# Differential attention on one core: the row squares taken earlier, the prompt's sums by products with ones, the last prompt one group sooner

## The chip, the core and the metric

The kernel runs on one core of a Trainium2 chip. Five engines work side by side, each through its own queue in order: TensorE (PE; its weight loads are shown apart as PEld), VectorE (DVE), ScalarE (ACT), GpSimd (POOL) and SyncE (SP), which issues most of the DMAs. The metric is the device time of one execution in microseconds (us); lower is better. The runs of the kernel before have a median of 2910.99 us.

## The reference, cut to what matters

One transformer layer for 256 prompt tokens and 2048 latent tokens, model width 1024. Attention has 4 heads; each head has two halves of 64 channels for queries and keys and one value of 128 channels. Latent queries read 512 cached and 2048 latent keys in one softmax; prompt queries read the 256 prompt keys.

```python
s = jnp.einsum('bqhmd,bkhmd->bhmqk', qblk, k).astype(jnp.float32) * scale
p = jax.nn.softmax(s, axis=-1)
a = p[:, :, 0] - lam * p[:, :, 1]                 # difference of the two halves
o = jnp.einsum('bhqk,bkhe->bqhe', a.astype(v.dtype), v)
...
a = rms_norm(attn, subln_g) * (1.0 - lam_init)    # per head, over its 128 channels
mix = jnp.concatenate([a.reshape(b, n, ATTN_WIDTH), four], axis=-1) @ w_out
x = x + g1 * mix
```

The per-head `rms_norm` is what most of the change is about: for every query the mean square over 128 channels of its output is needed.

## The kernel before

Before attention the kernel projects, normalises and rotates, and computes the Fourier half; after it come the out projection, and an MLP whose matmuls are combined so that seven products stand for eight. Between the parts there are no barriers: the work is one program, and attention's end overlaps the out projection's start.

**Attention.** `Head` holds the keys and values of one head, `Group` the work on 256 latent queries (two blocks j of 128), `Prompt` (a subclass of `Group`) that on the 256 prompt queries. There are 4 heads of 8 groups. All steps are put in a list with a time (`add(t, fn, ...)`, with T = 5.2 as the length of a row and u = T/5) and issued in the order of these times under `manual_schedule`; the times set the order alone. Synchronisation is derived from that order and from which tiles the instructions read and write.

A row of a group is one pass (j, half m) over the keys in blocks of 512:

- `fill`: two products give the scores of one block in a PSUM bank (L1081; tile S, five banks, tag "S").
- `rowmax` (L1086) takes the maximum of each block on VectorE, and `comb` (L1089) the maximum over the blocks.
- `exp` (L1105) on ScalarE writes the exponentials to SBUF (P0 or P1), and frees the bank. The scores of a row are made while the exponentials of the row before it are taken.
- `combine` (L1110 to L1121, VectorE and GpSimd) forms the difference of the two halves, scaled by the sums.

Six rows after its first, a group begins to turn its weights: `tr` transposes pairs of key blocks into a bank of tag "pt" (L1136; two banks), `ah` and `al` split them in a high and a low part (L1143 on ScalarE, L1148 on VectorE), and one row later `mul` multiplies them by the values (L1162 for the pairs kept in full precision, vf4 and vf14, and L95 to L97 for the others, three products each). The result gathers in columns 0 to 255 of one PSUM bank, po (`PRO()`), of which there is one.

When a group's products are complete, `o1` copies them to SBUF (oT, L1173), `o2` transposes them into columns 256 to 511 of the same bank (L1177), so that the queries lie on the partitions, and `o4` squares them with a sum along the row (L1183, two ACTIVATEs, each with a read of its accumulator). `o5` adds the epsilon term and raises to -1/2 on GpSimd (L1186, L92), `o6` and `o7` send the 256 numbers through DRAM to spread them over all partitions, `o8` (L1204) multiplies and `o9` (L1208) stores the group's output in `att`. Of the last group all from `o4` on is issued in the out projection (`LASTO`).

The prompt of a head runs between the rows of its groups 1 to 6, with scores and products in columns 256 to 511 of po. Its `o2` transposes into a bank of tag "pt" (L1265), and `o4` squares there (L1271).

In the times above, `o4` of a group stands at w + 8.5 u with w = base + 11 T + 1.0 u, which is 4.5 u into a row; the casts of that row (`ah`) stand at 3.3 and 3.8 u, and the value products of the following group (`mul`) at 3.9 u.

**The out projection** starts with 128 prompt tokens; their input mix0 is loaded by `mix0_load` (L1295) from `att[0]`, which the prompts of all four heads write, and split on VectorE (L1582, L1583).

Of the kernel before, what the change touches and what calls it, by code (L numbers as in the profile page):

```python
# [11 lines left out]
F32 = mybir.dt.float32  # L12
F32R = mybir.dt.float32r
AF = mybir.ActivationFunctionType
ALU = mybir.AluOpType
# [4 lines left out]
P = 128  # L20
# [6 lines left out]
H = 4  # L27
# [4 lines left out]
TSTEP, AVS = 5.2, 6  # L32
# [9 lines left out]
def body(tc, a, out):  # L42
    nc = tc.nc
    ctx = ExitStack()
    with ctx:
# [3 lines left out]
        def cst(name, shape, dt=F32):  # L49
            return const.tile(shape, dt, tag=name, name=name)  # L50
# [21 lines left out]
        ident = cst("ident", [P, P])  # L72
# [3 lines left out]
        ones = cst("ones", [P, 1])  # L76
# [14 lines left out]
        def pow_mhalf(dst, src, n):  # L91
            nc.gpsimd.tensor_tensor(dst, src, mhalf[:, :n], op=ALU.pow)  # L92
# [897 lines left out]
        with ExitStack() as c3_:  # L990
# [4 lines left out]
            at = c3_.enter_context(tc.tile_pool(name="a_t", bufs=2, reuse_waits="tile"))  # L995
# [4 lines left out]
            pT = c3_.enter_context(tc.tile_pool(name="a_pt", bufs=2, space=PSUM, reuse_waits="tile"))  # L1000
# [3 lines left out]
            @functools.cache  # L1004
            def PRO():

                return pPO.tile([P, 512], F32, tag="po", name="po")
# [32 lines left out]
            class Group:  # L1040
# [134 lines left out]
                def o2(self):  # L1175
                    for j in range(2):
                        nc.tensor.transpose(self.po[:, 256 + j * P:256 + j * P + P], self.oT[:, j * P:j * P + P], ident)  # L1177

                def o4(self):
                    osq = self.op.tile([P, P], F32, tag="osq", name=f"osq{self.nm}", bufs=1)  # L1180
                    self.oss = self.op.tile([P, 4], F32, tag="oss", name=f"oss{self.nm}")
                    for j in range(2):
                        nc.scalar.activation(osq, self.po[:, 256 + j * P:256 + j * P + P], AF.Square, accum_out=self.oss[:, j:j + 1])  # L1183

                def o5(self):
                    nc.gpsimd.tensor_add(self.oss[:, 0:2], self.oss[:, 0:2], self.s0e)  # L1186
                    pow_mhalf(self.oss[:, 2:4], self.oss[:, 0:2], 2)
# [22 lines left out]
            class Prompt(Group):  # L1210
# [47 lines left out]
                def o1(self):  # L1258
                    self.oT = f32(at.tile([P, 512], F32R, tag="ahp", name=f"oT{self.nm}", bufs=1))[:, 0:256]
                    nc.scalar.copy(self.oT, PRO()[:, 256:512])  # L1260

                def o2(self):
                    self.pt[1] = pT.tile([P, 512], F32, tag="pt", name=f"pt{self.nm}_o")[:, 0:256]
                    for j in range(2):
                        nc.tensor.transpose(self.pt[1][:, j * P:j * P + P], self.oT[:, j * P:j * P + P], ident)  # L1265

                def o4(self):
                    osq = at.tile([P, P], F32, tag="osq", name=f"osq{self.nm}", bufs=1)
                    self.oss = at.tile([P, 4], F32, tag="oss", name=f"oss{self.nm}")
                    for j in range(2):  # L1270
                        nc.scalar.activation(osq, self.pt[1][:, j * P:j * P + P], AF.Square, accum_out=self.oss[:, j:j + 1])  # L1271

            ev = []

            def add(t, fn, *args):
                ev.append((t, len(ev), fn, args))

            T = TSTEP
            u = T / 5.0
# [17 lines left out]
            for h in range(H):  # L1297
                hd, hp = Head(0, h), Head(1, h)
                base = h * 32 * T
                add(base - 18 * T + 0.7 if h else -3.04 * T, hd.load_k)  # L1300
                add(base - 14 * T + 0.7 if h else 0.9 * T, hd.load_v)
                add(base + 2 * T + 0.7, hp.load_k)
                add(base + 2 * T + 0.71, hp.load_v)
                gp = Prompt(hp, 0)
                G = [base + (AVS + 4 * g) * T for g in range(8)]
                add(G[1] - 3 * T, gp.qload)
                for j in range(2):
                    for m in range(2):
                        for t, fn in ((0.4, gp.scores), (0.85, gp.rowmax), (2.7, gp.exp)):
                            add(G[1 + 2 * j + m] + t * u, fn, j, m)  # L1310
                    add(G[2 + 2 * j] + 8 * u, gp.combine, j)
                for t, fn, *args in ((0.25, gp.tr, 0), (0.9, gp.ah), (1.4, gp.al), (17.0, gp.mul), (20.85, gp.o1), (24.2, gp.o2),
                                     (24.9, gp.o4), (25.6, gp.o5), (28.2, gp.o6), (32.7, gp.o7),
                                     (40.2, gp.o8), (43.0, gp.o9)):
                    add(G[5] + t * u, fn, *args)
                for g in range(hd.ng):
                    gr = Group(hd, g)
                    add(base - (4 if h or g > 1 else 3) * T + 0.6 * u if base else -3.03 * T, gr.qload)
                    for st in range(4):
                        j, m = divmod(st, 2)  # L1320
                        t0 = base + st * T
                        for b in range(hd.nbk):
                            add(t0 - T + (0.76 + 0.66 * b) * u, gr.fill, j, m, b)
                            add(t0 - T + (1.26 + 0.66 * b) * u, gr.rowmax, j, m, b)
                            add(t0 + 0.66 * b * u, gr.exp, j, m, b)
                        add(t0 - 0.45 * u, gr.comb, j, m)
                        if m:
                            add(t0 + (4.5 if gr.last and j else 5.9) * u, gr.combine, j)
                            if gr.last and j:
                                add(t0 + T + 5.3 * u, gr.combine_v, j)  # L1330
                    kbs = list(range(0, hd.nkt, 2))
                    for q in range(4):
                        w = base + (AVS + q) * T
                        if q % 2 == 0:
                            order = [kbs.pop(0) for _ in range(2)]
                            tr_t, ah_t, al_t = [0.7, 2.2], [3.3, 3.8], [4.6, 5.2]
                        else:
                            order = [kbs.pop(0) for _ in range(3)]
                            tr_t, ah_t, al_t = [0.7, 2.2, 3.86], [3.3, 3.8, 4.4], [None, 4.6, 5.2]
                        for n, kb in enumerate(order):  # L1340
                            add(w + tr_t[n] * u, gr.tr, kb)
                            add(w + (2.0 if gr.drain and kb == FULL[0] else ah_t[n]) * u, gr.ah, kb)
                            if al_t[n]:
                                add(w + al_t[n] * u, gr.al, kb)
                            add(w + T + (3.9 + 0.01 * n) * u, gr.mul, kb)
                            if q == 3 and not n:
                                add(w + 3.95 * u, gr.mul_part, kb)
                    w = base + (AVS + 5) * T + 1.0 * u
                    for t, fn in ((0, gr.o1), (0.4, gr.o2), (8.5, gr.o4), (9.2, gr.o5), (11.8, gr.o6), (16.3, gr.o7), (23.4, gr.o8), (26.0, gr.o9)):
                        if gr.last and t > 1:  # L1350
                            LASTO.append(fn)
                        else:
                            add(w + t * u, fn)
                    base += 4 * T
            add(base - 16 * T, load_wout)
            add(base + (AVS - 2) * T + 0.7 * u, mix0_load)
            with tc.manual_schedule():
                for _, _, fn, args in sorted(ev, key=lambda e: (e[0], e[1])):
                    fn(*args)
# [87 lines left out]
        WO5, HO, LO, hp = {}, {}, [], {}  # L1447
# [264 lines left out]
        with c5r, ExitStack() as c5:  # L1712
# [4 lines left out]
            PSB, U, G = {}, {}, {}  # L1717
# [152 lines left out]
            with tc.manual_schedule():  # L1870
                for n, (q, p) in enumerate(ITEMS):
# [21 lines left out]
                    ps = mms(q, p)  # L1893
                    fn, args = FINISH.get(n, (None, ()))
# [66 lines left out]
        with ExitStack() as c6:  # L1961
# [62 lines left out]
            with tc.manual_schedule():  # L2024
                pend, NM, loaded, KS = None, 7 * 24, 4, []
                for i in range(7):
                    for b in range(3):
                        ps = [pp.tile([P, 512], F32, tag="ps", name=f"ps{i}_{b}_{j}", bufs=6) for j in range(3)]
                        for k in range(16):
                            n, m = i * 16 + k, (i * 3 + b) * 8 + k // 2  # L2030
# [18 lines left out]
                            if (i, b) == (6, 2) and 9 <= k < 12:  # L2049

                                j = k - 9
                                u = U3[6 + j]
# [13 lines left out]
                for j in range(3):  # L2066
                    t = 6 + j
# [70 lines left out]
```

## Time and profile before

| | us |
|---|---|
| runs shown | 2908.22, 2910.99, 2912.67 (median 2910.99) |
| the profiled execution, its own time | 2909.53 |
| its span, first to last instruction | 2907.7 |
| granted TensorE clock over the span | 0.999 |

| engine | busy us | share of the span |
|---|---|---|
| PE | 2841.9 | 98% |
| PEld | 2446.2 | 84% |
| DVE | 1983.5 | 68% |
| ACT | 1535.3 | 53% |
| POOL | 1074.3 | 37% |

Attention's first combined maximum is at 520.75 us and its last at 1269.82; its last product ends at about 1297.

How to read the lines: a group of instructions is named by line, engine, operation, the tile written and the tiles read ("po<-ahs,Vs"), with buffer numbers left out; "s" at the end of a name is latent, "p" prompt. A line of the timeline starts with its start and its length in us; merged neighbours carry their count (x4). What stands in brackets is the idle time of the engine just before, and what ended it. A wait is put down to the releaser that came last. Matmuls are pipelined: a busy TensorE is not one at its peak, and the start of the weight load (PEld) is the sharper mark. L95 to L97 and L92 are lines of helpers.

### The profile page before, as it was taken

What the parts mean: (1) busy time and instruction counts of PE and PEld (TensorE: products, weight loads), DVE (VectorE), ACT (ScalarE), POOL (GpSimd) and SP (SyncE); (2) the same over time, 40 slices, a digit from 0 to 9 for tenths busy, and PEclk for the clock granted to TensorE, in tenths of its full rate; (3) what the DMA queues carried; (4) which work ended last, traced back from release to release, by engine and by line L of the source; (5) the groups of instructions that cost most, each with busy time, mean ns of one, the idle gap of its engine ahead of it and who ended that gap; (6) DMA issues with size and microseconds to landing.
All of it is one profiled execution on the core that took longest, in us unless ns stands there. A gap on an engine that the chain in (4) does not pass through costs nothing.

```text
span 2907.7 us, 42986 instructions
## 1 busy us (share of the span) xinstructions
PE 2841.9 (98%) x15021; PEld 2446.2 (84%) x15021; DVE 1983.5 (68%) x3321; ACT 1535.3 (53%) x3491; POOL 1074.3 (37%) x891
## 2 busy tenths in 40 slices
PE   8999999999999999999999999999999999999999
PEld 5888887677777777788889999999998888888887
DVE  7777787877777777775468778777775344345554
ACT  4333323888888888873346556556555332232221
POOL 1221124788888888862223333333332000000000
PEclk9999999999999999999999999999999999999999
DMA  7777767331222322326786667676656454445663
GB/s 281 215 213 205 225 205 248 142 109 45 77 73 52 109 35 50 95 57 205 222 267 208 224 227 242 225 240 221 218 193 245 149 186 153 137 146 178 205 211 109
DMA packets 404795, 497.69 MB, mean 171 GB/s; under 512 B 31539, under 2 KB 320672, under 8 KB 401506
## 3 DMA queue, kind: packets, MB, share of 16 engines
q1 hardware_dynamic: 399088, 484.35, 52.9%
q0 software_dynamic: 1936, 7.41, 0.8%
q10 hardware_dynamic: 3554, 3.17, 0.4%
q8 instruction: 119, 1.95, 0.3%
q14 instruction: 98, 0.80, 0.1%
HBM read 317.30 MB, written 179.62 MB: 171 GB/s over the span
## 4 chain that ended last, share of the span: by engine, by line
PE 53%; DVE 1%; DMA 0%; issue 0%; ACT 0%; POOL 0%; SPq 0%; DVEq 0%; POOLq 0%
PE ps L95 8%; PE ps L96 8%; PE ps L97 8%; PE pB L1755 2%; PE pB L1753 2%; PE pB L1754 2%; PE pA L1753 2%; PE pA L1754 2%; PE pC L1755 2%; PE pC L1753 2%; PE pA L1755 2%; PE pC L1754 2%; PE po L97 2%; PE po L95 2%; PE po L96 2%; PE pD L1755 1%
## 5 line engine op out<-in xcount | busy, mean ns | idle before, releaser
L1086 DVE TENSOR_REDUCE mxs<-Ss 128x1 f32<-128x512 f32 x636 | 410.6, 687 | 142.9 <-PE Ss L1081 135.5
L1430 DVE TENSOR_TENSOR sl<-sr,sh 128x768 fp32r<-128x768 f32 x168 | 161.8, 964 | 331.5 <-ACT sh L1429 331.1
L1121 POOL TENSOR_TENSOR P0s<-P0s,P1s 128x1024 f32<-128x1024 f32 (+2 forms) x128 | 377.5, 2949 | 10.7
L1429 ACT CAST sh<-sr 128x768 fp32r<-128x768 f32 x168 | 140.6, 838 | 418.2 <-PE ps L96 418.2
L1795 POOL TENSOR_TENSOR gs<-g,g 128x384 f32<-128x384 f32 x48 | 69.7, 1452 | 469.3 <-ACT g L1765 426.4
L1081 PE MATMUL Ss<-KS0s,Qs 128*128 128x512 f32 x636 | 201.6, 429 | 35.1 <-ACT P1s L1105 35.1
L95 PE MATMUL pj<-wh,hh 128*128 128x512 f32 x576 | 228.3, 396 | 2.3 <-DVE hh L556 2.0
L1105 ACT ACTIVATE P1s<-Ss,mxs 128x512 f32<-128x512 f32 x318 | 215.0, 696 | 25.5 <-DVE mxs L1089 24.5
L95 PE MATMUL ps<-thT,sh 128*128 128x512 f32 x585 | 227.6, 389 | 0.0
L96 PE MATMUL ps<-tlT,sh 128*128 128x512 f32 x585 | 227.6, 389 | 0.0
L97 PE MATMUL ps<-thT,sl 128*128 128x512 f32 x585 | 227.6, 389 | 0.0
L96 PE MATMUL pj<-wl,hh 128*128 128x512 f32 x576 | 226.8, 394 | 0.5 <-DVE wl L517 0.5
L97 PE MATMUL pj<-wh,hl 128*128 128x512 f32 x576 | 225.5, 392 | 0.0
L1105 ACT ACTIVATE P0s<-Ss,mxs 128x512 f32<-128x512 f32 x318 | 214.3, 691 | 5.1 <-DVE mxs L1089 4.0
L1136 PE MATMUL pts<-ident,P0s 128*128 128x128 f32 x1280 | 191.6, 273 | 5.1 <-DVE als L1148 2.0
L1081 PE MATMUL Ss<-KS1s,Qs 128*128 128x512 f32 x636 | 187.9, 419 | 1.8 <-ACT P0s L1105 1.4
L1136 PEld LDWEIGHTS pts<-ident,P0s 128*128 128x128 f32 x1280 | 151.2, 140 | 36.9 <-issue 4.6
L1764 ACT ACTIVATE g<-uz 128x384 f32<-128x384 f32 x144 | 75.7, 526 | 200.1 <-DVE uz L1787 173.7
L1120 POOL TENSOR_SCALAR P1s<-P1s,tots 128x1024 f32<-128x1024 f32 (+2 forms) x128 | 171.6, 1340 | 5.8
L1148 DVE TENSOR_TENSOR als<-pts,ahs 128x512 fp32r<-128x512 f32 x256 | 163.7, 681 | 8.2 <-ACT ahs L1143 8.1
L1081 PEld LDWEIGHTS Ss<-KS0s,Qs 128*128 128x128 f32 x636 | 97.6, 189 | 82.9 <-ACT P1s L1105 71.4
L95 PE MATMUL ps<-ophT,sh 128*128 128x512 f32 x423 | 164.7, 389 | 1.1 <-DVE uz L1787 1.1
(535 smaller groups left out, 8061.2 us busy)
## 6 DMA issues: line engine op xcount, KB each, us to landing
sr<-sd SPq DMA_DIRECT2D x84, 768.0 KB, 4.4
a<-in_w SPq DMA_DIRECT2D x184, 256.0 KB, 3.8
sd<-gs SPq DMA_DIRECT2D x192, 192.0 KB, 1.9
sd<-g SPq DMA_DIRECT2D x144, 192.0 KB, 4.0
wm<-in_w_mod SPq DMA_DIRECT2D x32, 512.0 KB, 5.3
Qs<-qd SPq DMA_DIRECT2D x32, 512.0 KB, 5.4
b<-in_w SPq DMA_DIRECT2D x64, 256.0 KB, 5.0
b<-tsum SPq DMA_DIRECT2D x64, 256.0 KB, 4.7
```

The lines of the kernel that those rows point to most:

```text
L95: nc.tensor.matmul(ps, lh, rh, start=first, stop=False)
L96: nc.tensor.matmul(ps, lh, rl, start=False, stop=False)
L97: nc.tensor.matmul(ps, ll, rh, start=False, stop=last)
L1081: nc.tensor.matmul(S[:, :w], self.Q[:, x, m, j * P:j * P + P], self.hd.KS[m][:, b * 512:b * 512 + w], start=(x == 0), stop=(x == 1))
L1086: nc.vector.tensor_reduce(self.mx[j][:, m, b:b + 1], self.S[j, m, b], axis=AX.X, op=ALU.max)
L1105: nc.scalar.activation(dst, S, AF.Exp, bias=self.mx[j][:, m, 6:7], accum_out=self.sm[j][:, m, b:b + 1])
L1120: nc.gpsimd.tensor_scalar(p, p, tot[:, 3:4], 0.0, op0=ALU.mult, op1=ALU.add)
L1121: nc.gpsimd.tensor_add(d, d, p)
L1136: nc.tensor.transpose(pt[:, c:c + P], self.p0[j][:, (kb + t) * P:(kb + t + 1) * P], ident)
L1753: nc.tensor.matmul(ps, wh[:, c], hh[:, k, :], start=first and k == 0, stop=False, skip_group_check=True)
L1754: nc.tensor.matmul(ps, wh[:, c], hl[:, k, :], start=False, stop=False, skip_group_check=True)
L1755: nc.tensor.matmul(ps, wl[:, c], hh[:, k, :], start=False, stop=k == 3, skip_group_check=True)
```

## The change

Four edits, all in attention's steps and their times:

1. `o4` of a latent group moves from w + 8.5 u to w + 7.85 u: 3.85 u into its row, behind the row's two casts and before the products of the following group (3.9 u), which write the other half of the bank that `o4` reads.
2. The prompt's sums of squares: a new step `oq` squares oT, the output with channels on the partitions, from SBUF into an SBUF tile (it takes the place of the buffer P1_1); `o2` is now two products of these squares with a column of ones, which sum over the partitions and give one number per query in a bank of tag "pt"; `o5` adds the epsilon term on VectorE, and `opow` raises to -1/2 on GpSimd. The transposes and the squares with accumulators go. The sums' store and load (`o6`, `o7`) stand 1.3 u later; `o8` and `o9` keep their times.
3. In the last head all steps of the prompt, its loads too, stand 4 T (one group) earlier.
4. `mix0_load` moves from 4 T + 0.7 u to 6.2 u behind the last group's rows.

```diff
+                def oq(self):
+                    self.osq = at.tile([P, 256], F32, tag="P1_1", name=f"osq{self.nm}", bufs=1)
+                    nc.scalar.activation(self.osq, self.oT, AF.Square)
+
                 def o2(self):
-                    self.pt[1] = pT.tile([P, 512], F32, tag="pt", name=f"pt{self.nm}_o")[:, 0:256]
+                    self.ps = pT.tile([P, 512], F32, tag="pt", name=f"ps{self.nm}")[:, 0:2]
                     for j in range(2):
-                        nc.tensor.transpose(self.pt[1][:, j * P:j * P + P], self.oT[:, j * P:j * P + P], ident)
-
-                def o4(self):
-                    osq = at.tile([P, P], F32, tag="osq", name=f"osq{self.nm}", bufs=1)
+                        nc.tensor.matmul(self.ps[:, j:j + 1], self.osq[:, j * P:j * P + P], ones, start=True, stop=True)
+
+                def o5(self):
                     self.oss = at.tile([P, 4], F32, tag="oss", name=f"oss{self.nm}")
-                    for j in range(2):
-                        nc.scalar.activation(osq, self.pt[1][:, j * P:j * P + P], AF.Square, accum_out=self.oss[:, j:j + 1])
+                    nc.vector.scalar_tensor_tensor(self.oss[:, 0:2], self.ps, 1.0, self.s0e, op0=ALU.mult, op1=ALU.add)
+
+                def opow(self):
+                    pow_mhalf(self.oss[:, 2:4], self.oss[:, 0:2], 2)
...
-                add(base + 2 * T + 0.7, hp.load_k)
-                add(base + 2 * T + 0.71, hp.load_v)
+                e = 4 * T * (h == H - 1)
+                add(base + 2 * T - e + 0.7, hp.load_k)
+                add(base + 2 * T - e + 0.71, hp.load_v)
...
-                for t, fn, *args in ((0.25, gp.tr, 0), (0.9, gp.ah), (1.4, gp.al), (17.0, gp.mul), (20.85, gp.o1), (24.2, gp.o2),
-                                     (24.9, gp.o4), (25.6, gp.o5), (28.2, gp.o6), (32.7, gp.o7),
+                for t, fn, *args in ((0.25, gp.tr, 0), (0.9, gp.ah), (1.4, gp.al), (17.0, gp.mul), (20.85, gp.o1), (24.45, gp.oq),
+                                     (25.3, gp.o2), (26.0, gp.o5), (26.05, gp.opow), (29.5, gp.o6), (34.0, gp.o7),
                                      (40.2, gp.o8), (43.0, gp.o9)):
-                    add(G[5] + t * u, fn, *args)
+                    add(G[5] - e + t * u, fn, *args)
...
-                    for t, fn in ((0, gr.o1), (0.4, gr.o2), (8.5, gr.o4), (9.2, gr.o5), (11.8, gr.o6), (16.3, gr.o7), (23.4, gr.o8), (26.0, gr.o9)):
+                    for t, fn in ((0, gr.o1), (0.4, gr.o2), (7.85, gr.o4), (9.2, gr.o5), (11.8, gr.o6), (16.3, gr.o7), (23.4, gr.o8), (26.0, gr.o9)):
...
-            add(base + (AVS - 2) * T + 0.7 * u, mix0_load)
+            add(base + 6.2 * u, mix0_load)
```

More of the change, by code (lines that the diff above doesn't have):

```diff
@@ L1301, in body @@
                 add(base - 14 * T + 0.7 if h else 0.9 * T, hd.load_v)
-                add(base + 2 * T + 0.7, hp.load_k)
-                add(base + 2 * T + 0.71, hp.load_v)
+                e = 4 * T * (h == H - 1)
+                add(base + 2 * T - e + 0.7, hp.load_k)
+                add(base + 2 * T - e + 0.71, hp.load_v)
                 gp = Prompt(hp, 0)
                 G = [base + (AVS + 4 * g) * T for g in range(8)]
-                add(G[1] - 3 * T, gp.qload)
+                add(G[1] - 3 * T - e, gp.qload)
                 for j in range(2):
@@ L1309, in body @@
                         for t, fn in ((0.4, gp.scores), (0.85, gp.rowmax), (2.7, gp.exp)):
-                            add(G[1 + 2 * j + m] + t * u, fn, j, m)
-                    add(G[2 + 2 * j] + 8 * u, gp.combine, j)
-                for t, fn, *args in ((0.25, gp.tr, 0), (0.9, gp.ah), (1.4, gp.al), (17.0, gp.mul), (20.85, gp.o1), (24.2, gp.o2),
-                                     (24.9, gp.o4), (25.6, gp.o5), (28.2, gp.o6), (32.7, gp.o7),
+                            add(G[1 + 2 * j + m] - e + t * u, fn, j, m)
+                    add(G[2 + 2 * j] - e + 8 * u, gp.combine, j)
+                for t, fn, *args in ((0.25, gp.tr, 0), (0.9, gp.ah), (1.4, gp.al), (17.0, gp.mul), (20.85, gp.o1), (24.45, gp.oq),
+                                     (25.3, gp.o2), (26.0, gp.o5), (26.05, gp.opow), (29.5, gp.o6), (34.0, gp.o7),
                                      (40.2, gp.o8), (43.0, gp.o9)):
-                    add(G[5] + t * u, fn, *args)
+                    add(G[5] - e + t * u, fn, *args)
                 for g in range(hd.ng):
```

## The prediction

> **What bounds the kernel now.** I read the page first (engine shares), then the waits of the attention stage, then the timeline of single rows in it, then windows from row to row. In the page's first part TensorE is nearly always busy, so a microsecond taken out of attention is not caught by slack later: the end moves only if TensorE moves.
>
> ```profile
> PE 2841.9 (98%) x15021; PEld 2446.2 (84%) x15021; DVE 1983.5 (68%) x3321; ACT 1535.3 (53%) x3491; POOL 1074.3 (37%) x891
> ```
>
> The change lies in attention, from 520 to 1300 us. I call a "row" the stretch from one combined maximum (DVE L1089) to the next: one exponential pass over 2560 keys for 128 queries. Waits of its regular part (574.49 to 1269.82 us: engine, tile, line, releaser: total, times, longest):
>
> ```profile
> PEld Ss L1081 <- ACT P1s L1105: 68.2, 114, 1.5
> ACT osqs L1183 <- PE po L97: 62.3, 29, 2.3
> PE Ss L1081 <- ACT P1s L1105: 34.7, 32, 1.2
> ACT osqp L1271 <- issue: 6.8, 3, 2.5
> ```
>
> ScalarE stands 29 times for 2.15 us before the squares of a group (L1183) until the value products (L97) end. What a row with that wait costs is in the windows; the columns are stretch: length, busy time of PE, PEld, DVE, ACT, POOL, then the granted clock, DMA share and GB/s:
>
> ```profile
> 914.43:919.78 5.35, 5.35 (x33) 4.32 (x32) 4.76 (x10) 4.61 (x13) 4.28 (x6) 1.00 0.07 25
> 919.78:926.97 7.19, 6.10 (x40) 4.70 (x39) 4.67 (x9) 5.47 (x17) 6.63 (x5) 1.00 0.00 1
> 932.33:938.02 5.69, 5.69 (x40) 4.64 (x40) 4.62 (x9) 5.06 (x14) 5.61 (x3) 1.00 0.66 194
> 689.51:697.31 7.80, 6.38 (x42) 4.86 (x42) 4.62 (x8) 5.74 (x18) 7.08 (x6) 1.00 0.03 5
> 883.12:890.68 7.56, 6.42 (x42) 4.90 (x42) 4.63 (x9) 5.75 (x18) 7.07 (x6) 1.00 0.02 2
> 1076.45:1083.99 7.54, 6.39 (x42) 4.88 (x42) 4.63 (x9) 5.75 (x18) 7.07 (x6) 1.00 0.01 0
> ```
>
> Every fourth row takes 7.19 us, its neighbours 5.35 to 5.69; the three rows below, one at the end of each of the first three heads, take 7.5 to 7.8: the prompt's squares (L1271) stand there in the same way. The timeline of the 7.19 us row shows the stall running round the engines:
>
> ```profile
> 917.95 1.09 ACT L1143 CAST ahs<-pts 128x512 fp32r<-128x512 f32 x2
> 918.49 0.85 PEld L1162 LDWEIGHTS po<-ahs,vf4s 128*128 128x128 f32 x4
> 919.78 0.16 DVE L1089 TENSOR_REDUCE mxs<-mxs 128x1 f32<-128x5 f32 x1
> 921.15 0.28 ACT L1183 ACTIVATE osqs<-po 128x128 f32<-128x128 f32 x1 [2.11 <-PE po L97]
> 921.72 0.19 ACT L1183 ACTIVATION_READ_ACCUMULATOR osqs<-po 128x1 f32 x1
> 921.81 0.68 ACT L1105 ACTIVATE P1s<-Ss,mxs 128x512 f32<-128x512 f32 x1
> 922.38 0.20 ACT L1105 ACTIVATION_READ_ACCUMULATOR P1s<-Ss,mxs 128x1 f32 x1
> 922.63 0.30 PEld L1081 LDWEIGHTS Ss<-KS0s,Qs 128*128 128x128 f32 x2 [1.33 <-ACT P1s L1105]
> 923.30 0.30 PEld L1081 LDWEIGHTS Ss<-KS0s,Qs 128*128 128x128 f32 x2 [0.37 <-ACT P1s L1105]
> 923.41 2.02 DVE L1086 TENSOR_REDUCE mxs<-Ss 128x1 f32<-128x512 f32 x3 [2.27 <-PE Ss L1081]
> 923.97 0.30 PEld L1081 LDWEIGHTS Ss<-KS0s,Qs 128*128 128x128 f32 x2 [0.37 <-ACT P1s L1105]
> 926.97 0.16 DVE L1089 TENSOR_REDUCE mxs<-mxs 128x1 f32<-128x5 f32 x1
> ```
>
> The squares read columns 256 to 511 of the PSUM bank po; the products write columns 0 to 255 of the same bank, and the read waits for them. So the order is kept per bank, not per column. While ScalarE waits, its exponentials are late, the score banks are not freed, TensorE waits 1.33 us and VectorE 2.27.
>
> **Part 1, a group's squares before the products (29 regular rows).** Nothing is removed; two ACTIVATEs with their reads move ahead of L1162/L95 to L97 of the same row, behind the second cast. The wait does not vanish, it turns round: now the products, which write the bank, must wait for the squares, and behind them on TensorE's queue stand the next row's transposes and score products, for which VectorE and ScalarE wait in turn. No row shows this order, since today the products never come close behind a read.
>
> On that the Trainium skill, page "PSUM — Partial Sum Buffer", section "PSUM bank collisions raise a hardware error", says that two engines may not touch one bank and quadrant at once, whichever columns, and that semaphores must guard by bank. By that rule this wait is compulsory; without it the sum would be the second rival's.
>
> Worked on the row above. The casts end at 917.95 + 1.09 = 919.04. The squares take 921.72 + 0.19 - 921.15 = 0.76, so they end at 919.80, or 919.65 if the first overlaps the last cast. A load on TensorE follows an accumulator read by 0.05 (922.58 to 922.63). The products' first load comes at 919.70 to 919.85 instead of 918.49: 1.21 to 1.36 late. From there to the next score load, an unblocked row tells:
>
> ```profile
> 907.45 0.64 PEld L1162 LDWEIGHTS po<-ahs,vf14s 128*128 128x128 f32 x4
> 908.74 0.16 DVE L1089 TENSOR_REDUCE mxs<-mxs 128x1 f32<-128x5 f32 x1
> 908.99 0.69 ACT L1105 ACTIVATE P1s<-Ss,mxs 128x512 f32<-128x512 f32 x1 [1.00 <-DVE mxs L1089]
> 910.03 0.30 PEld L1081 LDWEIGHTS Ss<-KS0s,Qs 128*128 128x128 f32 x2
> ```
>
> 2.58 us, plus 0.21 because the stretch on vf4s is 0.85 and not 0.64: 2.79. So the score load comes at 922.49 to 922.64, against 922.63 today: almost nothing is won there. What is won comes after it. The exponentials start 0.25 after the combined maximum (908.74 to 908.99), so at 920.03 instead of 921.81; the squares, done by 919.80, hide in the 1.00 us that ScalarE idles there anyway. The score banks are then free ahead of TensorE and the two gaps of 0.37 go. VectorE's first maximum follows the load by 0.78 (923.27 to 923.42); five of them back to back take 2.02 + 2 x 0.64 = 3.30, so the next combined maximum falls at 926.57 to 926.72 instead of 926.97. I take 0.35 a row (ends: 0, if the products' wait eats all; 0.75, if TensorE sets the pace and keeps both gaps). 29 x 0.35 = **10.2 us** (0 to 21.8).
>
> **Part 2, the prompt's sums.** Removed: two transposes and two squares that read PSUM. Added: one square of 128x256 from SBUF, two products of 128x128 with a column of ones, one small DVE add in place of a POOL add.
>
> ```profile
> 687.67 1.10 ACT L1143 CAST ahs<-pts 128x512 fp32r<-128x512 f32 x2
> 690.38 0.24 PEld L1265 LDWEIGHTS ptp_o<-ident,oTp 128*128 128x128 f32 x2
> 691.22 0.28 ACT L1271 ACTIVATE osqp<-ptp_o 128x128 f32<-128x128 f32 x1 [2.45 <-issue]
> 692.71 0.19 PEld L1081 LDWEIGHTS Ss<-KS0s,Qs 128*128 128x128 f32 x1 [1.31 <-ACT P1s L1105]
> L1173 ACT COPY oTs<-po x32: 367/372/378, 570.4 to 1296.9; 128x256 f32<-128x256 f32 x32
> ```
>
> The squares wait today because the transposes are queued on TensorE behind the products. The new square reads SBUF (written five microseconds before) and waits for nobody; priced by the copy of the same shape, 0.37, it ends at 688.77 + 0.37 = 689.14, before the maximum at 689.51, so ScalarE's idle time covers it (without the cover: 0.37 in each of four rows). The products with ones keep the transposes' place on TensorE, which is the path: two 128x128 loads, 0.24 by the transposes' row to 0.40 if a pipeline fill shows. The DVE add (0.16 by L1089) falls where VectorE waits for scores. POOL still makes the power behind its long add. So these rows come down to an unblocked 5.69 plus 0.24 to 0.40, say 6.05: 22.90 - 3 x 6.05 = **4.8 us** (3.5 to 5.2).
>
> **Part 3, the last head one group sooner, and the drain.** All the prompt's steps of that head move four rows earlier with their DMAs (two loads of K, V, Q, the sums' store and load, the output's store); their extra work on TensorE moves with them into rows of the same pattern, and SP passes them in the same places between the loads of Q, so I cost the move itself at nothing. On SP the load of mix0 moves ahead of the sums and stores of the last groups but one; it finds the prompt's output stored by then, so nothing queues behind it.  What the move is worth is in the drain:
>
> ```profile
> 1273.71 0.20 PEld L1177 LDWEIGHTS po<-ident,oTs 128*128 128x128 f32 x2 [2.00 <-ACT oTs L1173]
> 1289.12 0.58 ACT L1143 CAST ahs<-pts 128x512 fp32r<-128x512 f32 x1 [1.21 <-PE pts L1136]
> 1289.25 0.30 PEld L1162 LDWEIGHTS po<-ahs,vf4s 128*128 128x128 f32 x2
> 1297.33 0.69 DVE L1582 CAST mh<-wout 128x1024 fp32r<-128x1024 f32 x1 [1.72 <-DMA att<-oTs]
> ```
>
> The 2.00 us at 1273.71 come from the prompt's squares; 1.9 of them go. But two groups' squares are moved in front of products here too, where TensorE has no stall today: casts end at about 1290.2, squares at 1290.9, so the products of 1289.25 start some 1.6 late, and the pair before them likewise. 1.9 - 2 x 1.6 = -1.3. The input of the out projection (mix0) no longer comes last (1.72), but the later products eat part: +1.6. Then the half clock behind it:
>
> ```profile
> 921.00:924.41 3.41, 2.32 (x11) 1.29 (x10) 1.14 (x3) 3.23 (x12) 3.33 (x2) 1.00 0.01 2
> 1296.03:1299.44 3.41, 2.04 (x12) 1.20 (x11) 2.08 (x3) 2.55 (x8) 0.75 (x2) 1.00 0.91 252
> 1300.00:1302.00 2.00, 2.00 (x7) 1.61 (x6) 2.00 (x4) 2.00 (x5) 1.16 (x2) 0.50 0.70 115
> ```
>
> After 3.41 us with 2.04 of TensorE busy the granted clock is 0.50; if that lasts as long as the 3.41 before it, half of it, 1.7 us, is lost. An evener boundary spares it about as likely as not: 0.9. Together **1.2 us** (-1.5 to 3.5).
>
> **Sum.** 10.2 + 4.8 + 1.2 = 16.2 us off the profiled execution's 2909.53: 2893.3. That execution lies 1.5 under the median of the runs shown (2910.99), so I write 2894. Its own range, from the terms' likely ends: 2886 to 2902.
>
> **The rivals.**
> (a) The turned wait eats the row: part 1 is worth nothing, 4.8 + 1.2 = 6 us remain: 2904. For it: the score load moves by less than 0.15. Against: the two gaps and a ScalarE that is 1.8 us earlier. Chance 0.17.
> (b) The products don't wait. Then the score load falls at 918.49 + 2.79 = 921.28, the first maximum at 922.06, the combined one at 925.36: 1.6 a row, 29 x 1.6 = 46, plus 4.8 and some 4 at the drain: 2855. Against: the read waits for the other half of its bank today. Chance 0.05.
> (c) Slower, by the clock. The turned wait puts 1.2 to 1.4 us of idle time in one piece before the products. Today's rows hold 2.32 busy of 3.41 at clock 1.00; the boundary's 2.04 brought 0.50. If the new rows fall under the point between, 3.41 us at half clock cost 1.7 where a window of 3.41 covers the gap, (3.41 - 1.3)/3.41 = 0.6 of the rows: 29 x 0.6 x 1.7 = 30, and 2894 + 30 = 2924. Against: the gap it replaces is as long. Chance 0.08.
> The Trainium skill, page "TensorE: Matmul & The Clock Gate", section "HAM oscillation — how this bites in real kernels", asks only for no idle gap above about 3.4 us; by that (c) could not happen, yet the dip at 1300 came without any such gap.
> (d) It does not do what it says: a new stall (the bank of the new products, the earlier loads) returns the gain: 2910. Chance 0.08.
> The forecast keeps 0.62.
>
> **Range and chances.** 2880 to 2909 holds the forecast nearly whole, (a), and half of (d). What a measurement tells from no change is about 0.2%, 5.8 us, so faster is below 2905: 0.59 of the forecast, 0.10 of (a), (b): 0.74. Same: 0.17. Slower: (c) and a little of (d), 0.09.
>
> **What would show it.** Right: in the windows, every fourth row at 6.7 to 7.0; no ScalarE wait of L1183 on L97, and in its place 29 TensorE waits on L1183 of 1.2 to 1.4; ends of heads near 6.0. Wrong: rows at 5.5 (no wait, b), at 7.2 (a), or a granted clock under 1.00 inside attention (c).

## The result and the profile after

The changed kernel takes 2890.01 us (median of 6 runs, 2888.48 to 2891.93), the kernel before 2911.31 beside it (6 runs, 2908.22 to 2912.67): a ratio of 0.9928, 95% interval 0.9915 to 0.9941. Forecast were 2894 and 2880 to 2909. The profiled execution took 2891.27, with a span of 2889.5, against 2909.53 and 2907.7 before.

The page of the changed kernel, its first part (engine, busy us, share of the span, instructions):

```profile
span 2889.5 us, 42978 instructions
PE 2831.2 (98%) x15029; PEld 2452.5 (85%) x15029; DVE 1977.9 (68%) x3325; ACT 1538.7 (53%) x3479; POOL 1075.5 (37%) x887
```

TensorE's share of the span is what it was (98%). The waits of the changed kernel from 574.49 to 1250 us (engine, tile, line, releaser: total, times, longest):

```profile
ACT ahs L1143 <- PE pts L1136: 54.9, 87, 1.4
PEld po L1162 <- ACT osqs L1183: 37.9, 29, 1.3
PE po L1162 <- ACT osqs L1183: 25.3, 29, 0.9
PEld Ss L1081 <- ACT P1s L1105: 5.2, 25, 0.2
```

ScalarE no longer waits for the products before the squares. TensorE now waits 29 times for the squares instead, 37.9/29 = 1.31 us each. Its waits for free score banks (Ss, released by P1s), 68.2 us before, are down to 5.2. The windows of the same three rows as before (stretch: length; busy PE, PEld, DVE, ACT, POOL; clock, DMA share, GB/s), and of the ends of three heads:

```profile
906.26:911.62 5.36, 4.49 (x28) 3.18 (x26) 4.76 (x11) 5.25 (x17) 4.28 (x6) 1.00 0.07 24
911.62:918.19 6.57, 6.57 (x44) 5.94 (x45) 4.46 (x9) 4.94 (x13) 6.41 (x5) 1.00 0.00 0
923.55:929.24 5.69, 5.69 (x40) 4.65 (x40) 4.62 (x8) 5.06 (x14) 5.61 (x3) 1.00 0.83 206
690.37:696.37 6.00, 5.98 (x45) 5.35 (x44) 4.78 (x9) 5.12 (x14) 5.92 (x4) 1.00 0.04 12
877.29:883.29 6.00, 5.98 (x44) 5.36 (x44) 4.78 (x10) 5.13 (x14) 5.92 (x4) 1.00 0.03 6
1064.26:1070.26 6.00, 5.98 (x44) 5.36 (x44) 4.78 (x10) 5.13 (x14) 5.92 (x4) 1.00 0.17 17
```

The 7.19 us row takes 6.57, the ends of heads 6.00 each instead of 7.80, 7.56 and 7.54. Neighbours are unchanged (5.36, 5.69). The timeline of the row, to be laid beside the one in the prediction:

```profile
909.78 1.09 ACT L1143 CAST ahs<-pts 128x512 fp32r<-128x512 f32 x2
910.73 0.32 ACT L1183 ACTIVATE osqs<-po 128x128 f32<-128x128 f32 x1
911.35 0.19 ACT L1183 ACTIVATION_READ_ACCUMULATOR osqs<-po 128x1 f32 x1
911.59 0.73 PEld L1162 LDWEIGHTS po<-ahs,vf4s 128*128 128x128 f32 x4 [1.31 <-ACT osqs L1183]
911.62 0.16 DVE L1089 TENSOR_REDUCE mxs<-mxs 128x1 f32<-128x5 f32 x1
914.27 1.22 PEld L1081 LDWEIGHTS Ss<-KS0s,Qs 128*128 128x128 f32 x6
915.05 3.11 DVE L1086 TENSOR_REDUCE mxs<-Ss 128x1 f32<-128x512 f32 x5 [2.08 <-PE Ss L1081]
918.19 0.16 DVE L1089 TENSOR_REDUCE mxs<-mxs 128x1 f32<-128x5 f32 x1
```

The squares run from 910.73 to 911.54, close behind the casts, and the products' first weight load follows them by 0.05.

**Where the time went.** Adding the rows between combined maxima, from the thirteenth to the last: every fourth row sums to 193.6 us instead of 211.4 (17.8 saved over 29 rows), the ends of heads save 4.9. That is 22.7; the spans differ by 18.2. Given back in the profiled execution: 2.4 us in two early rows at half clock (last section), and 1.8 because attention's first combined maximum came at 522.5 instead of 520.75, a time that lies between 520.75 and 523.1 in the profiles taken here, whichever edit they hold, so it is not the change's doing. From the last combined maximum to the end of the span it is 1638.0 us, against 1637.9 before: the drain saved nothing.

### The profile page after: what moved, and what is told of

The parts are those of the page before. It is cut to its first block, busy times and chain, and to the rows that moved or that the text cites. A ratio compares the mean times of both kernels' runs of the same rounds, so it can differ in the third digit from the quotient of the medians.

```text
span 2889.5 us, 42978 instructions
## 1 busy us (share of the span) xinstructions
PE 2831.2 (98%) x15029; PEld 2452.5 (85%) x15029; DVE 1977.9 (68%) x3325; ACT 1538.7 (53%) x3479; POOL 1075.5 (37%) x887
## 4 chain that ended last, share of the span: by engine, by line
PE 54%; DVE 1%; issue 0%; ACT 0%; POOL 0%; DVEq 0%
PE ps L95 8%; PE ps L97 8%; PE ps L96 8%; PE pB L1761 2%; PE pB L1760 2%; PE pB L1759 2%; PE pA L1760 2%; PE pC L1760 2%; PE pC L1759 2%; PE pA L1759 2%; PE pA L1761 2%; PE pC L1761 2%; PE po L97 2%; PE po L96 2%; PE po L95 2%; PE pD L1761 1%
## 5 line engine op out<-in xcount | busy, mean ns | idle before, releaser
L1105 ACT ACTIVATE P1s<-Ss,mxs 128x512 f32<-128x512 f32 x318 | 215.4, 694 | 37.9 <-DVE mxs L1089 37.3
L1081 PE MATMUL Ss<-KS0s,Qs 128*128 128x512 f32 x636 | 190.4, 420 | 0.4 <-ACT P1s L1105 0.4
L1143 ACT CAST ahs<-pts 128x512 fp32r<-128x512 f32 x256 | 146.4, 606 | 60.4 <-PE pts L1136 60.4
```

Of the source, the lines that this page charges most:

```text
L1081: nc.tensor.matmul(S[:, :w], self.Q[:, x, m, j * P:j * P + P], self.hd.KS[m][:, b * 512:b * 512 + w], start=(x == 0), stop=(x == 1))
L1105: nc.scalar.activation(dst, S, AF.Exp, bias=self.mx[j][:, m, 6:7], accum_out=self.sm[j][:, m, b:b + 1])
```

## The experiments

Medians are of 4 to 10 runs, and every ratio is to the kernel before on the same chip, whose median lay between 2909.85 and 2911.16 us beside them.

| kernel | median us | ratio, 95% interval |
|---|---|---|
| the squares earlier, alone | 2895.41 | 0.9950 (0.9935 to 0.9965) |
| the prompt's sums, alone | 2905.55 | 0.9984 (0.9975 to 0.9993) |
| the shift and mix0, alone | 2912.00 | 1.0007 (0.9998 to 1.0016) |
| changed kernel without the shift | 2888.99 | 0.9926 (0.9911 to 0.9941) |
| changed kernel, squares at 7.6 u | 2873.89 | 0.9874 (0.9859 to 0.9889) |
| changed kernel, squares at 7.25 u | 2863.82 | 0.9839 (0.9822 to 0.9855) |
| changed kernel, squares at 2.35 u | 2863.31 | 0.9837 (0.9822 to 0.9852) |
| 7.25 u, late sums on POOL's queue | 2865.16 | 0.9851 (0.9835 to 0.9867) |
| 2.35 u, second input on ScalarE's queue | 2861.13 | 0.9828 (0.9814 to 0.9843) |
| the same without the shift | 2858.32 | 0.9818 (0.9801 to 0.9834) |

### Each part alone

The kernel before with one part of the change: the squares' time; the prompt's `oq`, `o2`, `o5`, `opow` and their times; the last head's `e` and the early `mix0_load`.

```diff
- (8.5, gr.o4)                       # squares alone
+ (7.85, gr.o4)
```

> The kernel before with one edit: the squares of a latent group at 7.85 u instead of 8.5 u. First theory (the turned wait is what is left of the row, the early exponentials are the gain): the row with the squares is 6.57 us as in the changed kernel, 29 x 0.62 = 18 us gained, the ends of heads stay at 7.5 to 7.8, and the drain loses about 1 by two waits of the products; total about 2894. Rival (the parts help each other, the prompt's new sums open the rows): the row stays above 6.8 and the total above 2900.

> The kernel before with the prompt's sums by products with ones alone (no earlier group squares, no shift of the last head, mix0 late). First theory: the ends of the first three heads come down from 7.5 to 7.8 to 6.0, the rows with the squares stay at 7.2, 1.9 more in the drain: 4.9 to 6.8 gained, total 2904 to 2906. Rival (the end of a head is short only because the rows around it are): under 3 gained.

> The kernel before with the last head's prompt one group sooner and the earlier load of mix0 alone. First theory: the prompt's stall moves from the drain into a row (7.5 instead of 5.7) and out of the drain (2.0), which cancel; mix0 no longer ends last, 0 to 1.7 gained: 2909 to 2911. Rival (the drain hides nothing of it): 3 or more gained.

Measured: 14.4 us saved by the squares, 4.3 by the sums, 2.1 lost by the shift (by its interval between 0.6 us gained and 4.7 lost, so no sure difference). In the first the squares' rows take 6.57 and the ends of heads still 7.5 to 7.6; in the second the ends of heads take 6.00 and the squares' rows 7.22. So each part acts in its own rows and not in the other's, with the sizes seen in the whole.

For the shift 2909 to 2911 was expected, and 2912.0 came. The prompt's stall moved into a row as expected (7.57 us where 5.7 stood), but the drain got no shorter for it: from the last combined maximum to the end 1638.6 us, against 1637.9 before.

In its drain stands a stall of its own, by its waits from 1250 to 1330 us:

```profile
PEld po L95 <- issue: 2.8, 1, 2.8
PE po L95 <- DVE mh L1583: 2.4, 1, 2.4
```

TensorE stands 2.8 us before the products of the out projection's second input. The same stall returns below, larger.

### The whole without the shift

```diff
- e = 4 * T * (h == H - 1)
+ e = 0
...
- add(base + 6.2 * u, mix0_load)
+ add(base + (AVS - 2) * T + 0.7 * u, mix0_load)
```

> The changed kernel without the last head's shift and with the late load of mix0: the group's squares and the prompt's sums alone. First theory (the shift is worth its drain: the prompt's steps out of the way and mix0 not last): 2 to 5 slower than the changed kernel, 2892 to 2895. Rival (the shift alone cost 2, so it costs 2 here too): 2886 to 2889.

2888.99 against 2890.01, and against the kernel before on the same chip each gains 21.3 us: the shift is worth nothing in the whole either. The squares and the sums together gain 2.6 us more than the 14.4 and 4.3 that each gains alone. In the profiles 1.2 of that lies in the drain. With the squares alone it is 1640.0 us long, since the prompt's stall (1.98 us) and the two turned waits (1.63 each) stand in it side by side; with the sums alone it is 1637.3, with both 1638.1. The squares alone also have an early row that is 1.1 longer at half clock (last section), in rows that no edit touched.

### Where the squares stand in the row

If the row's length hangs on TensorE's wait for the bank, it must follow the squares' end. The changed kernel, with the squares between the two casts (7.6 u), ahead of both (7.25 u), and one row earlier (2.35 u):

```diff
- (7.85, gr.o4)
+ (7.6, gr.o4)      # or 7.25, or 2.35
```

> The changed kernel with the group's squares at 7.25 u: same row, but ahead of the row's two casts on ScalarE, not behind them. First theory (the products' wait on the squares, 1.3 us in 29 rows, still sets the length of the row): the squares end about 0.95 sooner, the wait shrinks to 0.3 or 0.4, the row from 6.57 to 5.6 to 5.8, 22 to 28 us gained on the changed kernel: 2863 to 2868. Rival (that wait is covered, VectorE or ScalarE sets the row now): the row stays at 6.5 and the total at 2888 to 2891; or the casts, 0.76 later, cost what is won.

> The changed kernel with the group's squares at 2.35 u: a row earlier, in the row of the transposes they read, between its first and second cast. First theory (the products wait only for as long as the squares end after the score products): in that row the squares end about when the products are due, so the row of 5.69 grows by 0 to 0.3; the row after next comes down from 6.57 to 5.4 or 5.5; total as with the squares ahead of the casts or a little less, 2858 to 2868. Rival (ScalarE is full in that row, with three casts): that row grows by the whole 0.76 of the squares, total 2875 to 2885.

> The changed kernel with the group's squares at 7.6 u: between the row's two casts. First theory (row length follows the end of the squares one to one): they end one cast stagger, 0.47, sooner, the products' wait goes from 1.31 to about 0.85, the row from 6.57 to 6.1, 29 x 0.47 = 13.6 gained on the changed kernel: about 2876. Rival (a threshold, all or nothing): like the changed kernel, 2888 to 2891, or like the squares ahead of both casts, 2864.

The timeline and then the windows of one such row with the squares ahead of both casts:

```profile
894.01 0.30 ACT L1183 ACTIVATE osqs<-po 128x128 f32<-128x128 f32 x1
894.60 0.19 ACT L1183 ACTIVATION_READ_ACCUMULATOR osqs<-po 128x1 f32 x1
894.69 1.06 ACT L1143 CAST ahs<-pts 128x512 fp32r<-128x512 f32 x2
894.84 0.73 PEld L1162 LDWEIGHTS po<-ahs,vf4s 128*128 128x128 f32 x4 [0.34 <-ACT osqs L1183]
```

```profile
890.48:895.84 5.36, 5.36 (x32) 4.06 (x31) 4.76 (x11) 5.24 (x17) 4.92 (x6) 1.00 0.07 24
895.84:901.49 5.65, 5.65 (x41) 5.11 (x40) 4.47 (x8) 4.84 (x13) 5.57 (x3) 1.00 0.00 0
```

Between the casts, one row's windows and the waits of the regular part (576 to 1230 us):

```profile
901.95:908.03 6.08, 6.08 (x43) 5.48 (x43) 4.46 (x9) 4.95 (x13) 5.96 (x4) 1.00 0.00 0
```

```profile
PEld po L1162 <- ACT osqs L1183: 23.8, 29, 0.8
```

| squares | median row | wait of the products, each |
|---|---|---|
| behind both casts (7.85 u) | 6.58 | 1.31 |
| between them (7.6 u) | 6.12 | 0.82 |
| ahead of both (7.25 u) | 5.63 | 0.33 |
| one row earlier (2.35 u) | 5.44 | under 0.2, in 24 rows |

In the first three the row shortens by 0.46 and 0.49 as the wait shortens by 0.49 each time. That is one for one, and it settles the cause: what holds the row is the products' wait for the squares' read of the bank, not the clock (1.00 in all of them) and not ScalarE's load, whose instructions are the same. The casts need not come first: ahead of both, the squares put them off from 3.52 to 4.21 us behind the combined maximum, and the rows show nobody who is later for that. So the change left some 25 us of the same gain unused: it gains 21.3 us on the kernel before, and 46.0 with the squares ahead of the casts. One row earlier there is nothing more to win: the squares' row falls to 5.44, but the row before it grows from 5.36 to 5.47 (it is this row that grows, not the row of 5.69 as expected), and the medians lie 0.5 us apart.

### The boundary behind it

With the squares early, the drain got longer: from the last combined maximum to the end 1640.7 us with the squares ahead of the casts, against 1638.0. Its timeline there, VectorE, TensorE and SP's queue (SPq, DMA issues):

```profile
1250.34 0.32 SPq L1199 DMA_DIRECT2D rbs<-rs  x1
1250.71 0.43 SPq L1581 DMA_DIRECT2D mT<-att  x1
1257.03 0.69 DVE L1588 CAST mh<-mT 128x1024 fp32r<-128x1024 f32 x1 [4.81 <-DMA mT<-att]
1257.84 0.29 PEld L95 LDWEIGHTS po<-woh,mh 128*128 128x128 f32 x1 [4.85 <-issue]
```

The second input's load (mT) is issued right behind the load of a late group's sums, and TensorE waits 4.85 us for what it brings. Behind that wait the granted clock is 0.50 from 1256.07 to 1262.89. Two ways to free it: the late groups' stores and loads on POOL's queue, or the two loads of mT on ScalarE's.

```diff
- return nc.gpsimd if self.last else nc.sync, ...
+ return nc.gpsimd if self.last or self.drain else nc.sync, ...
```

> The kernel with the squares ahead of the casts (7.25 u), and the sums and the output of the last group but one sent by GpSimd's queue instead of SyncE's, as those of the last group are. First theory (with faster rows the 4.85 us wait of TensorE at the out projection's second input is SyncE's queue, held by that group's chain of stores and loads): the wait falls below 1, and 2 to 3 of half clock behind it goes too; 3 to 6 gained on 2864: 2858 to 2861. Rival (the input's own transfer is slow, whoever issues it): no gain, 2862 to 2866.

```diff
- def mix_load(i):
+ def mix_load(i, q=nc.sync):
...
- mix_load(s1)
+ mix_load(s1, nc.scalar)
```

> The kernel with the squares at 2.35 u, and the two loads of the out projection's second input (mT) issued on ScalarE's queue instead of SP's. There TensorE stood 4.6 us (4.9 on VectorE's cast) for this input, because its loads were issued on SP at 1250.54, behind a group's sums and store. Theory (the order on SP is the cause, and nothing else is as late): the loads are issued near 1240, the wait goes, 2863.3 - 4 = 2859 us. Rival (another input of the boundary is as late, as when the sums went to POOL): the mT wait goes, a new wait of 3 to 5 us stands behind it, 2862 to 2864 us.

> The same, with the last head's prompt and the load of mix0 back at their old times. If the shift is worth nothing here either (as between the changed kernel and the one without its shift, where it cost 1 us), the time is within 2 us of the kernel with the shift. If the shift frees the boundary once the second input is not late, it is 2 to 4 us slower.

On POOL's queue the wait for mT goes, and no time is won (2865.16). Its timeline:

```profile
1272.47 0.72 POOL L1204 TENSOR_TENSOR oTs<-oTs,rbs 128x256 f32<-128x256 f32 x1 [4.76 <-DMA rbs<-rs]
1274.10 0.58 POOL L92 TENSOR_TENSOR nrsb<-nssb,mhalf 128x1 f32<-128x1 f32 x1
1274.72 0.75 DVE L236 TENSOR_SCALAR xn<-xo,nrsb 128x1024 f32<-128x1024 f32 x1 [6.49 <-POOL nrsb L92]
1275.53 1.57 PEld L249 LDWEIGHTS ptb<-ident,xn 128*128 128x128 f32 x8 [6.81 <-DVE xn L236]
```

POOL waits 4.76 us for the sums' round trip through DRAM, the power of the next norm stands behind it on POOL, and TensorE waits 6.81 us for that norm. On ScalarE's queue nothing of this kind stands behind the loads, and the wait for mT is gone too. But the waits from 1235 to 1285 us of that kernel show:

```profile
DVE gt L1607 <- DMA g<-gate: 5.3, 2, 3.0
PEld ptb L249 <- DVE xn L236: 4.1, 1, 4.1
```

TensorE again stands before the norm, 4.1 us, and 3.4 in the version without the shift (1.0 where the mT wait was). The rival of that expectation came: another input is as late. VectorE stands twice (2.95 and 2.38 us) for the loads of the gates (g), which SP issues at 1257.27, behind a late group's store; from the second wait on it works without a pause up to the sum that the norm needs. With mT on SP these loads are issued at 1252.98, and VectorE does not wait for them.

The half clock moves along with the wait. It now lies behind the norm: from 1273.63 to 1280.46 on POOL's queue, from 1275.23 to 1278.64 on ScalarE's. From the norm's first transposes to the end these two take 1586.7 and 1586.2 us, against 1584.6 where mT is late.

On ScalarE's queue some 2 us of the 4 expected are left in the medians. Without the shift it was 2.8 us quicker still, where a difference under 2, or a loss, was expected. The intervals of the three kernels overlap: whether the queue is worth anything isn't settled. The quickest kernel measured is the one with the squares at 2.35 u, the second input on ScalarE's queue and no shift: 2858.32 us, 0.9818 (0.9801 to 0.9834) of before, some 32 us below the changed kernel.

## Why the prediction was right

**The total.** 2894 was forecast and 2890.0 measured. The sum was 16.2 us; the two profiled executions differ by 18.3, and the medians by 21.3. (2893.3 and the 1.5 make 2894.8; the prediction wrote 2894.) That the total came so near is in part luck: the rows saved 22.7 us where parts 1 and 2 had 15.0, part 3 brought nothing where it had 1.2, and the profiled execution gave back 4.2 in two places that the sum does not have.

**Part 1, mechanism right, size too small.** The wait turned round as worked out: 29 waits of 1.31, forecast 1.2 to 1.4. Counted from the row's combined maximum, the products' load comes at 5.33 us instead of 4.06, 1.27 late (forecast 1.21 to 1.36), and the score load at 8.01 instead of 8.20 ("almost nothing is won there"). Two terms were mis-sized: from the products' load to the score load 2.68 us where 2.79 was taken, and the five maxima 3.11 where 3.30 was taken. So a row gains 0.62 (7.19 to 6.57) and not 0.35; 29 rows gave 17.8 us, not 10.2, inside the stated 0 to 21.8. The sign "every fourth row at 6.7 to 7.0" was missed by the same amount.

**Part 2, right.** 6.05 was forecast for the ends of heads and 6.00 measured, 4.9 us against 4.8. The groups of the new operations in the changed kernel, 570 to 1300 us (busy, mean ns of one, idle before):

```profile
L1264 ACT ACTIVATE osqp<-oTp 128x256 f32<-128x256 f32 x4 | 1.9, 472 | 0.0
L1269 PEld LDWEIGHTS psp<-ones,osqp 128*128 128x128 f32 x16 | 2.1, 190 | 0.0
L1269 PE MATMUL psp<-ones,osqp 128*128 128x1 f32 x16 | 2.0, 230 | 0.0
```

The square takes 0.47 us and not the copy's 0.37, hidden as said. The copy that it reads ends 2.8 us before it, not five, and that is early enough. Four weight loads stand for each pair of products where I had counted two; the row still came out 0.31 above an unblocked one (5.69), inside the 0.24 to 0.40.

**Part 3, the price of the drain right, its gain not there.** The changed kernel from 1245 to 1300 us, waits:

```profile
PEld po L1162 <- ACT osqs L1183: 3.3, 2, 1.6
PEld po L97 <- DVE ml L1589: 1.0, 1, 1.0
```

The two turned waits cost 3.3 us, as the 2 x 1.6 in the sum. VectorE waits for mix0 no more. Still, the out projection's first product starts 28.9 us after the last combined maximum, against 28.3 before: 0.6 lost up to there, where -1.3 + 1.6 had promised 0.3. Without the shift and the early mix0 it starts 29.1 us after; so the squares and the sums lost 0.8 there, and the two other edits brought back 0.2. Then the half clock, gone in the changed kernel, should bring 1.7. But the first transposes of the MLP's norm begin at 1304.9, 53.4 us after that maximum in both kernels, and TensorE waits longer for them:

```profile
PEld ptb L249 <- DVE xn L236: 2.0, 1, 2.0
```

That wait was 1.1 before, so 0.9 of the 1.7 went into it, and what was left no more than made good the 0.6 lost ahead of it. The steps that failed are "the input of the out projection (mix0) no longer comes last", of whose +1.6 only 0.2 arrived at the first product, and "+0.9" for the clock, half of which the next dependent chain took. The term of 1.2 measured 0, and the shift by itself -2.1 (alone) and 0 (in the whole, 21.3 with it and without it), the first not surely different from nothing either.

**The rivals.** (a) asked for a row of 7.2, and (d) for the gain returned by a new stall; neither came. (b), products that don't wait, is out by the 29 waits; but its price for the stall, 1.6 us a row, is what moving the squares ahead of the casts brought (7.20 to 5.63), by shortening the wait and not by its absence. The products and the squares use two halves of one tile (po), between which the program itself keeps the order, and no run leaves that wait out; so its price is shown here, and not whether the chip would need it. I took the place behind the casts as given and did not ask what an earlier one would bring. (c): in the squares' rows the clock stays at 1.00, with 1.31 us of idle time in one piece. Its point between 2.04 and 2.32 us busy is not in the traces either: in the kernel before, 1.96 us busy from 507.55 to 510.96 are followed by a clock of 1.00.

## What to carry to other kernels

Where the program orders a read and a write of one bank, turning their order need not remove the stall: here its new length was the time from when the writer could start to when the reader ended, and the row followed it one for one. So put the read ahead of work on its engine that nobody waits for yet, and try the places before and behind it. At the seam of two stages, ask which chain is late next before a freed wait is counted as won: here the next norm, or a queue in order, took most of it back.

## What was not expected of the hardware

The half clock came back in a place that was left alone: in two early rows of attention. Windows of the changed kernel:

```profile
541.02:544.43 3.41, 1.92 (x9) 1.11 (x9) 2.74 (x7) 3.41 (x12) 3.33 (x3) 1.00 0.01 2
544.43:547.84 3.41, 3.41 (x13) 2.68 (x11) 1.98 (x3) 3.16 (x10) 3.33 (x2) 0.50 0.00 0
547.84:551.25 3.41, 1.57 (x11) 1.07 (x9) 2.78 (x6) 1.73 (x4) 3.15 (x5) 1.00 0.37 141
551.25:554.66 3.41, 3.41 (x13) 2.73 (x11) 1.99 (x3) 2.80 (x9) 3.41 (x2) 0.50 0.06 20
```

And of the kernel before, the same work:

```profile
541.68:545.09 3.41, 2.65 (x15) 2.00 (x16) 1.90 (x6) 3.41 (x12) 3.33 (x3) 1.00 0.00 0
545.09:548.51 3.42, 1.58 (x11) 1.03 (x10) 3.10 (x6) 2.40 (x7) 3.24 (x4) 1.00 0.40 116
548.51:551.92 3.41, 3.41 (x20) 2.46 (x20) 2.65 (x5) 3.22 (x10) 3.33 (x3) 1.00 0.12 44
```

Twice in the changed kernel a stretch with under 2 us of TensorE busy is followed by one at 0.50. In the kernel before, the first of its stretches holds 2.65, because the same idle time lies across its edge; but then 1.58 busy is followed by 1.00. So the busy share of the stretch before does not decide alone: the half-clock stretches of one profile start whole multiples of 3.41 us apart, and on that grid, from 500 to 1310 us in the twelve profiles, a stretch with under 1.5 us of TensorE busy is always followed by 0.50, but one with 1.56 to 2.1 sometimes by 0.50 and sometimes by 1.00. What else decides stays open. The Trainium skill, page "TensorE: Matmul & The Clock Gate", section "A second HAM failure mode: psum-queue depth-cycling", describes for another kernel a clock that goes down and up because TensorE idles briefly and often between groups of matmuls. By that such dips are possible, and the trace agrees as far as no idle time of TensorE's matmuls in these rows is longer than 1.84 us.

Dips in the early rows stand in three profiles (the changed kernel, the squares alone, the second input on ScalarE's queue) and not in those of the kernel before and the other eight experiments, although these rows hold the same instructions in the same order in all twelve kernels, with the same longest idle time (1.84 to 1.85 us). So the edits did not touch these rows. The dips cost 1.0 and 1.4 us in the changed kernel's profile, less than the 3.45 us between its shortest and longest run.
